# First halves of two units' states moved ahead of a scan's end, in an S5 + SwiGLU layer on one Trainium2 core

## The chip, the cores and the metric

The kernel runs on one core of one Trainium2 chip. The metric is the device time of one execution in microseconds (us); of several executions the median is taken. The engines are TensorE (PE; its weight loads are listed as PEld), VectorE (DVE), ScalarE (ACT), GpSimd (POOL) and SyncE (SP, which only issues DMA transfers here). ACT and POOL issue DMA transfers too; such an issue is listed under the engine's queue (ACTq, SPq).

## The reference, cut to what matters

The layer takes 1024 latent tokens and 256 context tokens of 1024 channels. It normalises and modulates them, runs a bidirectional S5 mixer, applies GELU and a gated linear unit (GLU), adds the residual, and then runs a SwiGLU feed-forward block (FFN) and a last norm. The S5 mixer has 64 groups of 16 channels; each group has 64 complex states per direction:

```
def run(u, h0):
    bu = jnp.einsum('lgh,gnh->lgn', u, b_bar)
    bu = bu.at[0].add(lam_bar * h0)
    a = jnp.broadcast_to(lam_bar, bu.shape)
    _, h = lax.associative_scan(_linear_combine, (a, bu), axis=0)
    return jnp.einsum('lgn,ghn->lgh', h, c_mat).real, h[-1]
...
fc, fl = s5_direction(uc, ul, *p_fwd)
bc, bl = s5_direction(uc[::-1], ul[::-1], *p_bwd)
...
y = y + d_skip * h;  g = gelu(y);  out = g * sigmoid(g @ w_glu + b_glu)
```

The scan must finish before the last tokens of either direction have their states; GELU, the GLU and the FFN follow.

## The kernel before

**Tiling.** Eight neighbouring tokens make one column: 32 context columns and 128 latent ones. Within a column the eight tokens act on each other through a small lag matrix (a Toeplitz block); between columns only the states are carried. The 64 groups make eight units of eight groups, two units to each of four quarters q. `STQ[q]` holds the states of a quarter: 160 columns, real and imaginary part, 16 entries, of which eight belong to each unit. The output of unit k is the sum of two products on TensorE: the lag product of its inputs (`x_mm`, lines 940 to 950, weights `KQ`) and the products of its states with the matrices `CL[q]` (`states_mm`, line 925, for half of the 128 columns; `states_all`, line 938, for all).

**The scan.** `scan()` runs on VectorE, in 32 steps over odd columns 33 to 95 (two columns at a time) and then 63 steps over every column to 158. A step is two products and two sums, each for all quarters. The even columns up to 94, left out by the first 32 steps, are filled afterwards by `rot`: two products and two sums on 128x64 elements (four columns of one unit). The procedure `one()` takes one such operation from a list after each of the two sums of a step, so a step has two slots. The list holds quarters 0 and 2. GpSimd fills quarters 1 and 3 (`fill`, letter F), whole, in eight operations for each half.

**The order.** Everything around and behind the scan is written out by hand in two strings of short words, PROG1 and PROG2, which `run` executes word by word; each engine then works through its own instructions in that order. The letters that matter here:

- C: one of four parts of `CL[q]`, two products on GpSimd and a sum, which the table HOWS puts on GpSimd (E) or on TensorE with ScalarE copying the result back (P, line 672). C32 and C33 are the last two parts of quarter 3.
- K: the lag products of half a quarter (`k_mats`, lines 812 to 820) into the banks `kt` and `pm`, two copies on ScalarE (line 824) and two writes to DRAM from ScalarE's queue.
- T: a load of one `KQ` from there, on SyncE's queue (line 833).
- R, Z, z: a copy of the backward states in turned order: first half (R, line 905, ScalarE), last half (Z) or both (z, line 907 on VectorE, line 905 on ScalarE).
- P: `x_mm` and the first half's states of a unit, into two of three banks `pw`. Y: the copy of the result into `Y` (line 996, ScalarE).
- N: the last half's states; D: VectorE adds them to `Y`. H: GELU. Q: for units 6 and 7, `x_mm` and both halves' states at once.
- I, J: transposes of `Y` for the GLU (line 1054) with the copy and the subtraction that split them in two parts; g: products of the GLU (lines 1095 to 1097).

PROG1 stands beside the scan and PROG2 behind it, and between the two all PSUM pools are closed and a new one (`pe`, eight banks) is opened. Units 0 to 5 have their first half in PROG1; units 6 and 7 come whole in PROG2.

Of the kernel before, what the change touches and what calls it, by code (L numbers as in the profile page):

```python
# [13 lines left out]
AF = mybir.ActivationFunctionType  # L14
# [3 lines left out]
P = 128  # L18
# [24 lines left out]
def s5_ffn_kernel(tc, a, out):  # L43
# [3 lines left out]
    with ctx:  # L47
# [879 lines left out]

        def states_all(k, pts, hs):

            for a_ in range(4):  # L930
                for ri in range(2):
                    for d in range(2):
                        for c in range(2):
                            cs_ = slice(64 * c, 64 * c + 64)
                            for gp in range(2):
                                ps = slice(64 * gp, 64 * gp + 64)
                                st = hs[ps, cs_, ri, a_] if d else STQ[k // 2][ps, 31 + 64 * c:95 + 64 * c, ri, 8 * (k % 2) + a_]
                                PE.matmul(flat(pts[gp][cs_, a_]), st, flat(CL[k // 2][ps, ri, d, 4 * (k % 2) + a_]),
                                          start=False, stop=a_ + ri + d == 5)

        def x_mm(k, pool):
# [10 lines left out]
        inner = {}  # L952
        HSe = [view(r, kb, [64, 2, 4]) for r, kb in ((RC[3], 14), (RC[3], 12), (RC[3], 14), (RC[3], 12), (RA, 2), (RA, 0))]
        HSl = [view(RA, STB * (i // 3) + 4.125 + 2 * (i % 3), [64, 2, 4]) for i in range(6)]
        HSq = {6: view(RA, 0, [P, 2, 4]), 7: view(RA, STB, [P, 2, 4])}

        def run(prog):


            for w in prog.split():  # L960
# [18 lines left out]
                elif op == "F":  # L979
                    fill(*divmod(i, 10), *((RW, 0) if i >= 30 else (RC[3], 12)))  # L980
                elif op == "T":
# [3 lines left out]
                elif op == "Z":  # L985
                    turned(i, 1, HSl[i], ENG[ZEN[i]])
                elif op == "z":
                    turned(i, 2, HSq[i], ENG[ZEN[i]])
                elif op == "P":
                    inner[i] = x_mm(i, pw)  # L990
                    states_mm(i, inner[i], 0, HSe[i], False)
                elif op == "Q":
                    inner[i] = x_mm(i, pe8)
                    states_all(i, inner[i], HSq[i])
                elif op == "Y":
                    S.copy(yview(i // 2, i % 2), inner[i // 2][i % 2])
                elif op == "N":
                    late[i] = [pe8([4, T, HC]) for _ in range(2)]
                    states_mm(i, late[i], 1, HSl[i], True)
                elif op == "D":  # L1000
                    for gp, po in enumerate(late[i]):
                        tt(yview(i, gp), po, yview(i, gp), ADD)
                elif op == "H":
                    if i in late:
                        S.activation(Y[:, i], Y[:, i], AF.Gelu_apprx_tanh)
                    else:
                        for gp in range(2):
                            S.activation(yview(i, gp), inner[i][gp], AF.Gelu_apprx_tanh)
                elif op == "I":
# [761 lines left out]
```

## Time and profile before

| | |
|---|---|
| median of 3 runs | 1016.06 us (1015.48 to 1016.09) |
| profiled execution | 1014.43 us |
| its span, first to last instruction | 1012.6 us |
| mean granted TensorE clock | 0.988 |
| busy: PE, DVE, POOL, ACT | 960.8, 778.9, 761.1, 438.5 us |

The profiled execution is 1.8 us longer than its span. A granted clock of 1.00 is TensorE's full 2.4 GHz and 0.50 is 1.2 GHz. The trace shows two records for each matmul on these 32-bit numbers: the 32 matmuls of half a unit's states are 64 records. The record of a matmul contains its way out of the array, so that neighbouring records overlap; the time that a series takes is read from start to start.

### The profile page before, as it was taken

The numbers are of one execution on the slowest core, as the hardware profiler recorded it, in microseconds if no ns is written. First come the engines' busy times: TensorE is split into PE (matmuls) and PEld (weight loads), VectorE is DVE, ScalarE is ACT, GpSimd is POOL, SyncE is SP. The second block draws the span as 40 slices with busy tenths as digits, with TensorE's granted clock in tenths as the row PEclk, the third lists the DMA queues.
The fourth block names the chain that finished last, engine by engine and source line by source line (L and its number), as shares of the span: only waits on it lengthen the run. The fifth ranks groups of instructions, "written<-read, shape, count | busy, mean of one in ns | idle before, by whom it ended". The sixth has DMA issues, their size and how long they took to land. (4 is left out here: it accounts for less than half of the span.)

```text
span 1012.6 us, 18558 instructions
## 1 busy us (share of the span) xinstructions
PE 960.8 (95%) x6988; PEld 771.8 (76%) x6988; DVE 778.9 (77%) x1642; ACT 438.5 (43%) x858; POOL 761.1 (75%) x586
## 2 busy tenths in 40 slices
PE   5987799799999999999999999999999999999996
PEld 1465423589999988778888888888888888888885
DVE  7979799995366867877958677686958677686987
ACT  5487622325444663443343343324343343424337
POOL 5799899993662448979785878777786877777774
PEclk9999999898999999999999999999999999999999
DMA  9765997324512021011212111121212111121205
GB/s 336 280 135 98 312 325 240 95 80 138 188 48 79 1 105 63 28 44 45 73 42 83 42 52 42 50 66 53 73 42 83 43 47 47 45 70 53 73 22 166
DMA packets 48546, 98.96 MB, mean 98 GB/s; under 512 B 4284, under 2 KB 18876, under 8 KB 47176
## 3 DMA queue, kind: packets, MB, share of 16 engines
q1 hardware_dynamic: 43272, 86.64, 25.7%
q0 software_dynamic: 2016, 7.34, 3.8%
q10 hardware_dynamic: 3168, 3.79, 1.1%
q8 instruction: 55, 0.90, 0.4%
q14 instruction: 35, 0.29, 0.1%
HBM read 84.25 MB, written 6.17 MB: 89 GB/s over the span
## 5 line engine op out<-in xcount | busy, mean ns | idle before, releaser
L77 POOL TENSOR_TENSOR c<-rxc,c 128x512 fp32r<-128x512 f32 x128 | 166.6, 1316 | 53.5 <-ACT c L1225 52.6
L1285 PE MATMUL ut<-ra,c 128*128 128x512 f32 x400 | 155.7, 389 | 1.2 <-DVE ra L77 1.2
L1284 PE MATMUL ut<-ra,c 128*128 128x512 f32 x400 | 155.7, 389 | 0.2 <-ACT ra L1225 0.2
L1286 PE MATMUL ut<-ra,c 128*128 128x512 f32 x400 | 155.6, 389 | 0.0
L1225 ACT CAST c<-rxc 128x512 fp32r<-128x512 f32 x128 | 79.0, 622 | 146.7 <-PE xt L1579 53.3
L1579 PE MATMUL xt<-c,c 128*128 128x512 f32 x540 | 129.7, 389 | 0.0
L77 DVE TENSOR_TENSOR ru<-ru,xt 128x1024 f32<-128x1024 f32 x90 | 107.9, 1216 | 13.4 <-PE xt L1579 9.4
L1579 PEld LDWEIGHTS xt<-c,c 128*128 128x128 f32 x540 | 101.4, 188 | 21.0
L77 DVE TENSOR_TENSOR ru<-ut,ru 128x512 f32<-128x512 f32 x98 | 67.2, 686 | 43.0 <-PE ut L1286 37.5
L1285 PEld LDWEIGHTS ut<-ra,c 128*128 128x128 f32 x400 | 75.1, 188 | 17.1 <-POOL rxc L77 1.5
L1284 PEld LDWEIGHTS ut<-ra,c 128*128 128x128 f32 x400 | 75.1, 188 | 16.1 <-ACT ra L1225 0.6
L1286 PEld LDWEIGHTS ut<-ra,c 128*128 128x128 f32 x400 | 75.1, 188 | 15.5
L77 POOL TENSOR_TENSOR c<-rw,c 128x512 fp32r<-128x512 f32 (+1 forms) x29 | 39.8, 1373 | 37.5 <-ACT c L1225 37.5
L77 POOL TENSOR_TENSOR c<-ru,c 128x512 fp32r<-128x512 f32 (+1 forms) x39 | 58.8, 1507 | 10.1 <-ACT c L1225 5.7
L1284 PE MATMUL ut<-c,c 128*128 128x512 f32 x160 | 62.3, 390 | 0.8 <-DVE rxa L77 0.8
L77 POOL TENSOR_TENSOR rxc<-rxc 128x512 f32<-128x512 f32 x40 | 61.5, 1537 | 1.6
L1286 PE MATMUL ut<-c,c 128*128 128x512 f32 x160 | 62.3, 389 | 0.0
L1285 PE MATMUL ut<-c,c 128*128 128x512 f32 x160 | 62.2, 389 | 0.0
L1579 PE MATMUL ut<-c,c 128*128 128x512 f32 x216 | 51.9, 389 | 0.0
L77 DVE TENSOR_TENSOR pe<-pe,ru 128x256 f32<-128x256 f32 x64 | 27.4, 428 | 29.5 <-ACT pe L1125 17.4
L584 PE MATMUL pv<-ru,c 128*64 128x160 f32 x512 | 42.3, 305 | 7.2 <-POOL ru L77 2.5
L77 DVE TENSOR_TENSOR ru<-ru,ut 128x512 f32<-128x512 f32 x76 | 47.3, 681 | 0.3
(440 smaller groups left out, 2571.2 us busy)
## 6 DMA issues: line engine op xcount, KB each, us to landing
c<-in_ada_w SPq DMA_DIRECT2D x46, 256.0 KB
rxc<-in_w SPq DMA_DIRECT2D x38, 256.0 KB
rxc<-in_w SPq DMA_DIRECT2D x19, 512.0 KB
ru<-in_w SPq DMA_DIRECT2D x11, 512.0 KB
rw<-in_w SPq DMA_DIRECT2D x11, 512.0 KB
ra<-in_ada_w SPq DMA_DIRECT2D x10, 512.0 KB
ra<-in_ada_w SPq DMA_DIRECT2D x18, 256.0 KB
ru<-in_xT SPq DMA_DIRECT2D x4, 1024.0 KB
```

Of the source, the lines that this page charges most:

```text
L77: eng.tensor_tensor(out=o, in0=x, in1=y, op=op)
L584: PE.matmul(pv[64 * (i % 2):64 * (i % 2) + 64, ri, c0:c0 + 160], w[:, i, 64 * ri:64 * ri + 64], U[:, 8 * b + 4 * j + i], start=True, stop= ...
L1225: S.copy(o[0], x)
L1284: PE.matmul(pu, wh, bh, start=start, stop=False)
L1285: PE.matmul(pu, wh, bl, start=False, stop=False)
L1286: PE.matmul(pu, wl, bh, start=False, stop=stop)
L1579: PE.matmul(pd, w[:, cs_], b, start=j in (1, 2, 4) and n == 0, stop=n == 2, skip_group_check=j not in (1, 2, 4))
```

## The change

- PROG1 gains the first half's states of units 6 and 7: new words R6, p6, Y12, Y13 and R7, p7, Y14, Y15. The word p is `states_mm` without `x_mm`. Unit 7's result goes to a place of its own (`Y7`), since `Y` still lies over inputs that unit 6 needs.
- In PROG2 units 6 and 7 go through N and D: N is `x_mm` and the last half's states for these two, D the sum on VectorE, H one GELU. Q, z, `states_all` and `HSq` go. The buffers of the turned states get new places (`HSe`, `HSl`), of which some are shared by R and Z words.
- F30 and F31 go. Of quarter 3's fills, unit 6's and the first half of unit 7's go into the scan's slots (12 more fills, 48 operations), behind quarter 2's, which now run unit by unit; the rest is f7, four operations on GpSimd behind C33.
- The sum of C32 goes from GpSimd to TensorE (HOWS).
- K3 stands directly behind K2; unit 2's `x_mm` (X2) ahead of K4 and K5, its states (S2) behind them; K6 ahead of p7 and K7 behind Y15; M2 and m0 (modulation columns) ahead of R5; T12 to T15 at the end of PROG1.

```
-HOWS = "PPPP PPEE PEEE EEEE"
+HOWS = "PPPP PPEE PEEE EEPE"
 PROG1, from M1 on:
-K2 R0 P0 Y0 Y1 K3 L3 R1 C20 P1 Y2 Y3 T4 T5 G3 T6 T7 C21 C22 C23 K4 K5 R2 P2 Y4 Y5 R3 P3 Y6 Y7 T8 T9 T10 T11
-C30 C31 R4 P4 Y8 Y9 C32 C33 R5 P5 Y10 Y11 K6 K7 M2 m0 F30 F31
+K2 K3 R0 P0 Y0 Y1 L3 R1 C20 P1 Y2 Y3 T4 T5 G3 T6 T7 C21 C22 C23 R2 X2 K4 K5 S2 Y4 Y5 R3 P3 Y6 Y7 T8 T9 T10 T11
+C30 C31 R4 P4 Y8 Y9 C32 C33 f7 M2 m0 R5 P5 Y10 Y11 R6 p6 Y12 Y13 R7 K6 p7 Y14 Y15 K7 T12 T13 T14 T15
 PROG2:
-Z0 N0 Z1 Z2 D0 Z3 N1 D1 Z4 H0 H1 N2 D2 H2 T12 T13 T14 T15 N3 Z5 D3 H3 N4 D4 z6 z7 I0 J0 I1 J1 ... Q6 H6 I4 J4 Q7 b0 I5 J5 H7 g03 ...
+Z0 N0 Z1 Z2 D0 Z3 N1 D1 Z4 H0 H1 N2 D2 H2 N3 Z5 D3 H3 N4 D4 Z6 Z7 I0 J0 I1 J1 ... N6 D6 H6 I4 J4 N7 D7 b0 I5 J5 H7 g03 ...
@@ scan
-            for j in range(8):
-                for d in range(2):
-                    rest.extend(fill_ops(2, d, j))
+            for k in range(4, 8):
+                for j in range(4 if k == 7 else 8):
+                    rest.extend(fill_ops(k // 2, k % 2, j))
@@ run
+                elif op == "f":
+                    fill(i // 2, 1, RW, 0, (8 * (i % 2),))
+                elif op == "p":
+                    inner[i] = [pw([4, T, HC]) for _ in range(2)]
+                    states_mm(i, inner[i], 0, HSe[i], True)
-                elif op == "Q":
-                    inner[i] = x_mm(i, pe8)
-                    states_all(i, inner[i], HSq[i])
-                    late[i] = [pe8([4, T, HC]) for _ in range(2)]
-                    states_mm(i, late[i], 1, HSl[i], True)
+                    late[i] = x_mm(i, pe8) if i > 5 else [pe8([4, T, HC]) for _ in range(2)]
+                    states_mm(i, late[i], 1, HSl[i], i < 6)
```

## Rows read from the trace of the kernel before

**Rows 1.** Busy time of each engine by stage (us, PE, PEld, DVE, ACT, POOL, PEclk, DMA)

```profile
228.00:262.00 34.00, 33.55 (x773) 32.55 (x761) 15.06 (x25) 15.72 (x23) 15.08 (x13) 0.92 0.57 174
...
360.00:470.00 110.00, 107.54 (x479) 88.08 (x478) 84.35 (x133) 48.72 (x90) 85.77 (x61) 1.00 0.18 63
470.00:1000.00 530.00, 530.00 (x2340) 438.84 (x2339) 401.11 (x472) 204.21 (x362) 403.68 (x300) 1.00 0.17 56
```

**Rows 2.** Timeline of DVE in the scan (start, us, engine, line, operands)

```profile
127.09 0.30 DVE L77 TENSOR_TENSOR ltb<-ra,lta 128x128 f32<-128x128 f32 x1
...
128.14 0.30 DVE L77 TENSOR_TENSOR ltb<-ra,lta 128x128 f32<-128x128 f32 x1
...
132.34 0.29 DVE L77 TENSOR_TENSOR ltb<-ra,lta 128x128 f32<-128x128 f32 x1
...
133.39 0.29 DVE L77 TENSOR_TENSOR ltb<-ra,lta 128x128 f32<-128x128 f32 x1
...
226.65 0.29 DVE L77 TENSOR_TENSOR ra<-ltc,ra 128x128 f32<-128x128 f32 x1
```

**Rows 3.** Groups of DVE instructions, 127 to 227 us (busy, mean ns, idle before)

```profile
L77 DVE TENSOR_TENSOR ltb<-ra,lta 128x128 f32<-128x128 f32 x95 | 27.4, 288 | 1.1
...
L77 DVE TENSOR_TENSOR lta<-ra,lta 128x64 f32<-128x64 f32 x64 | 13.8, 215 | 0.0
```

**Rows 4.** Timeline of ACT: copies of R5, of P5's, K6's and K7's results

```profile
218.61 0.63 ACT L905 COPY ra<-ra 128x512 f32<-128x512 f32 x1
222.35 1.07 ACT L996 COPY ru<-pw 128x512 f32<-128x512 f32 x2 [3.10 <-PE pw L925]
224.00 0.36 ACT L824 COPY r<-kt 128x240 f32<-128x240 f32 x1 [0.57 <-PE pm L820]
...
228.42 0.36 ACT L824 COPY rw<-kt 128x240 f32<-128x240 f32 x1 [3.31 <-PE pm L820]
```

**Rows 5.** PE by source line in short stretches: L938, L948, L925, L672 (us, PE, PEclk, DMA)

```profile
247.00:251.40 4.40, 4.25 (x128) 1.00 0.00 0
...
245.00:247.10 2.10, 1.93 (x16) 1.00 0.20 74
...
220.00:222.40 2.40, 2.28 (x64) 1.00 0.48 172
...
183.00:187.00 4.00, 3.70 (x8) 1.00 0.29 82
```

**Rows 6.** Timeline of DVE: sums D0, D1, D2 behind N0, N1, N2

```profile
232.59 1.29 DVE L77 TENSOR_TENSOR ru<-pe,ru 128x512 f32<-128x512 f32 x2 [3.66 <-PE pe L925]
...
235.03 1.29 DVE L77 TENSOR_TENSOR ru<-pe,ru 128x512 f32<-128x512 f32 x2 [0.82 <-PE pe L925]
237.01 1.29 DVE L77 TENSOR_TENSOR ru<-pe,ru 128x512 f32<-128x512 f32 x2 [0.69 <-PE pe L925]
```

**Rows 7.** PE alone, one us at a time (us, PE busy, PEclk, DMA)

```profile
194.00:195.00 1.00, 0.00 (x0) 1.00 0.57 173
...
196.00:197.00 1.00, 0.63 (x66) 0.52 0.09 25
...
226.00:227.00 1.00, 0.17 (x9) 0.88 0.38 124
```

**Rows 8.** Groups of PE instructions, 195 to 262 us (busy, mean ns, idle before)

```profile
L948 PE MATMUL pw<-ra,ru 128*128 128x128 f32 x64 | 10.7, 324 | 2.1 <-issue 1.4 <-ACT ru L996 0.7
...
L812 PE MATMUL kt<-c,rxa 64*16 64x112 f32 x120 | 6.1, 300 | 4.7 <-POOL c L77 3.5 <-ACT r L824 0.9 <-issue 0.3
```

**Rows 9.** Timeline of POOL: the sums of C32 and C33, and F31's last two

```profile
212.03 2.37 POOL L77 TENSOR_TENSOR c<-c,ra 128x1024 f32<-128x1024 f32 x1
...
218.45 2.38 POOL L77 TENSOR_TENSOR c<-c,rw 128x1024 f32<-128x1024 f32 x1
...
231.68 1.54 POOL L77 TENSOR_TENSOR ra<-ra,rw 128x256 f32<-128x256 f32 x2
```

**Rows 10.** Timeline of SP's queue: T12 to T15

```profile
231.30 4.16 SPq L833 DMA_DIRECT2D ra<-kd  x4
```

More of the change, by code (lines that the diff above doesn't have):

```diff
@@ L29 @@
 MAGIC = 12582912.0
-HOWS = "PPPP PPEE PEEE EEEE"
+HOWS = "PPPP PPEE PEEE EEPE"
 ZEN = "VVSVSVSV"
-PROG1 = ("A22 B0 A26 C02 G1 A30 A34 C03 A40 K0 A44 A48 C10 K1 L2 A54 G2 C11 A60 F10 C12 F11 C13 T0 T1 T2 T3 A64 M0 M1 K2 R0 P0 Y0 Y1 K3 L3 R1 C20 P1 Y2 Y3 T4 T5 G3 T6 T7 C21 C22 C23 K4 K5 R2 P2 Y4 Y5 R3 P3 Y6 Y7 T8 T9 T10 T11 C30 C31 R4 P4 Y8 Y9 C32 C33 R5 P5 Y10 Y11 K6 K7 M2 m0 F30 F31")
-PROG2 = ("Z0 N0 Z1 Z2 D0 Z3 N1 D1 Z4 H0 H1 N2 D2 H2 T12 T13 T14 T15 N3 Z5 D3 H3 N4 D4 z6 z7 I0 J0 I1 J1 w0 w1 l1 H4 N5 D5 I2 J2 H5 I3 J3 W0 W1 x0 x1 x2 x3"
-         " Q6 H6 I4 J4 Q7 b0 I5 J5 H7 g03 g13 I6 J6 g23 g05 g15 I7 J7 V1 w20 w21 g26 x10 x11 x12 x13")
+PROG1 = ("A22 B0 A26 C02 G1 A30 A34 C03 A40 K0 A44 A48 C10 K1 L2 A54 G2 C11 A60 F10 C12 F11 C13 T0 T1 T2 T3 A64 M0 M1 K2 K3 R0 P0 Y0 Y1 L3 R1 C20 P1 Y2 Y3 T4 "
+         "T5 G3 T6 T7 C21 C22 C23 R2 X2 K4 K5 S2 Y4 Y5 R3 P3 Y6 Y7 T8 T9 T10 T11 C30 C31 R4 P4 Y8 Y9 C32 C33 f7 M2 m0 R5 P5 Y10 Y11 R6 p6 Y12 Y13 R7 K6 p7 Y14 Y15 K7 T12 T13 T14 T15")
+PROG2 = ("Z0 N0 Z1 Z2 D0 Z3 N1 D1 Z4 H0 H1 N2 D2 H2 N3 Z5 D3 H3 N4 D4 Z6 Z7 I0 J0 I1 J1 w0 w1 l1 H4 N5 D5 I2 J2 H5 I3 J3 W0 W1 x0 x1 x2 x3"
+         " N6 D6 H6 I4 J4 N7 D7 b0 I5 J5 H7 g03 g13 I6 J6 g23 g05 g15 I7 J7 V1 w20 w21 g26 x10 x11 x12 x13")
 LOG2E = 1.4426950408889634
@@ L867, in scan, with fill @@
                 one()
-        def fill(q, h, reg, kb):
+        def fill(q, h, reg, kb, es=(0, 8)):
             tmps = [view(reg, kb + i, [256]) for i in range(2)]
             st, c0 = STQ[q], 32 * h
-            for e in (0, 8):
+            for e in es:
                 rot(st[:, 32 + c0:63 + c0:2, :, e:e + 8], st[:, 31 + c0:62 + c0:2, :, e:e + 8], LS[:, 0], 16 * q + e, E, tmps)
@@ L926, in states_mm @@
                                       start=start and ri == 0, stop=ri == 1 and (start or a_ == 3))
[L928 to L939, printed above, removed]
         def x_mm(k, pool):
@@ L952, in s5_ffn_kernel @@
         inner = {}
-        HSe = [view(r, kb, [64, 2, 4]) for r, kb in ((RC[3], 14), (RC[3], 12), (RC[3], 14), (RC[3], 12), (RA, 2), (RA, 0))]
-        HSl = [view(RA, STB * (i // 3) + 4.125 + 2 * (i % 3), [64, 2, 4]) for i in range(6)]
-        HSq = {6: view(RA, 0, [P, 2, 4]), 7: view(RA, STB, [P, 2, 4])}
+        HSe = [view(r, kb, [64, 2, 4]) for r, kb in ((RC[3], 14), (RC[3], 12), (RC[3], 14), (RC[3], 12), (RA, 2), (RA, 0), (RA, 4), (RA, 6))]
+        HSl = [view(RA, (4, 6, 0)[i] if i < 3 else STB * (i // 3) + 4.125 + 2 * (i % 3), [64, 2, 4]) for i in range(8)]
+        Y7 = [view(RA, 8 + 2 * i, [4, T, HC]) for i in range(2)]
         def run(prog):
@@ L986, in run @@
                     turned(i, 1, HSl[i], ENG[ZEN[i]])
-                elif op == "z":
-                    turned(i, 2, HSq[i], ENG[ZEN[i]])
                 elif op == "P":
@@ L991, in run @@
                     states_mm(i, inner[i], 0, HSe[i], False)
-                elif op == "Q":
-                    inner[i] = x_mm(i, pe8)
-                    states_all(i, inner[i], HSq[i])
+                elif op == "X":
+                    inner[i] = x_mm(i, pw)
+                elif op == "S":
+                    states_mm(i, inner[i], 0, HSe[i], False)
+                elif op == "p":
+                    inner[i] = [pw([4, T, HC]) for _ in range(2)]
+                    states_mm(i, inner[i], 0, HSe[i], True)
                 elif op == "Y":
-                    S.copy(yview(i // 2, i % 2), inner[i // 2][i % 2])
+                    S.copy(Y7[i % 2] if i > 13 else yview(i // 2, i % 2), inner[i // 2][i % 2])
                 elif op == "N":
-                    late[i] = [pe8([4, T, HC]) for _ in range(2)]
-                    states_mm(i, late[i], 1, HSl[i], True)
+                    late[i] = x_mm(i, pe8) if i > 5 else [pe8([4, T, HC]) for _ in range(2)]
+                    states_mm(i, late[i], 1, HSl[i], i < 6)
                 elif op == "D":
                     for gp, po in enumerate(late[i]):
-                        tt(yview(i, gp), po, yview(i, gp), ADD)
+                        tt(yview(i, gp), po, Y7[gp] if i == 7 else yview(i, gp), ADD)
                 elif op == "H":
[L1004 to L1008, printed above, removed]
+                    S.activation(Y[:, i], Y[:, i], AF.Gelu_apprx_tanh)
                 elif op == "I":
```

2 lines of the change are left out of this document (1 added, 1 removed).

## The prediction

> **What bounds the kernel now.** I read the busy time by stage first. From 470 to 1000 us TensorE is busy all 530.00 us, from 360 to 470 it misses 2.5 us, from 228 to 262 it misses 0.45 [rows 1]. Behind about 228.8 us, then, the time is the moment at which TensorE begins PROG2 plus the work it has from there on; a microsecond of TensorE work taken out behind that point is a microsecond of the result, and what VectorE, ScalarE and GpSimd do there has room.
>
> Next I asked the timelines what sets that moment. VectorE's scan begins at 127.09 and its last sum ends at 226.65 + 0.29 = 226.94: 95 steps [rows 2, 3] of 1.051 us, without a gap. N0 needs the last columns and Z0, a copy that takes VectorE not quite 1 us more, so 228 is the earliest. TensorE itself is then busy with K7; its copy out of bank `kt` runs at 228.42 for 0.36 us [rows 4], and N0 begins right behind it, at 228.83. So two chains end almost together: the scan (228.0) and TensorE's queue in PROG1 (228.8). Work moved from behind the join to ahead of it is free only as far as that second chain has slack.
>
> **The change part by part.**
>
> *The states taken out of PROG2.* A Q issues 64 state matmuls, 4.25 us; half of them, as P and N have, take 2.28 (64 records) [rows 5]. Both numbers hold the same way out of the array, so the difference, 1.97, is clean. Two units: -3.9 us behind the join. The lag products (1.93 us each, 16 records [rows 5]) stay there. D6 and D7 are new on VectorE, 1.29 us each [rows 6], and H6 and H7 wait for them; what needs H6 and H7 are I6 and I7, which stand behind N7 and several g words, so TensorE has other work. Z6 and Z7 copy half of what z6 and z7 copied. Cost on the path: nothing; if that cover were gone, 1.3 us a unit.
>
> *The clock behind the join.* N0's result reaches VectorE at 232.59, N1's at 235.03, N2's at 237.01 [rows 6]: 3.7, 2.4 and 2.0 us. In the 1 us table the granted clock drops during 226 to 227, when TensorE had worked 0.17 us of that microsecond [rows 7]; the stage's mean is 0.92 [rows 1]. So N0 and part of N1 ran at 1.2 GHz, and against N2's 2.0 they lost 1.7 + 0.4 = 2.1 us. In the new order p6, K6, p7 and K7 follow each other with no wait of theirs longer than about 1.7 us, and the clock should be at full when N0 begins: -2.1. Bounds: 0 (it drops anyway) and -2.1; I take -2.1, because what stood ahead of the drop, a queue of K6 and K7 that waited for each other's banks, is now filled by p7.
>
> *The start of N0.* I add up TensorE's queue ahead of the join. Up to K4 little changes: K4 waits 3.5 us for GpSimd's last part of quarter 2 [rows 8], with TensorE idle from 192 to 195 [rows 7], and X2 (1.9 us) fits in that hole. K3 directly behind K2 has to wait for K2's copies, about 2 us, which the same hole takes up. With X2 gone from behind K5, and the clock not down (it fell at 196, right after the hole [rows 7], and units 2's and 3's products ran slow), P4 should end about 211.5.
>
> C32 then needs GpSimd's products. GpSimd's sum of C32 began at 212.03 [rows 9], so they are there at 212.0, and nothing ahead of them on GpSimd is changed. From there: C32's sum on TensorE 3.5 (a sum of this kind: 3.70 with its tail [rows 5]); P5 4.1 (1.9 + 2.2); then a hole, since p6 has no lag products to cover the copies ahead of it on ScalarE: Y10 and Y11 1.07 and R6 0.63 [rows 4], 1.7; p6 2.0; K6 1.7 (from the end of P5's states, just ahead of the copies at 222.35, to 224.00 [rows 4]); p7 2.1; K7 1.7; its first copy 0.4. 212.0 + 17.2 = 229.2. C33 on GpSimd ends 2.37 earlier, at 218.4 instead of 220.8, ahead of p6, which needs it, and f7 (four operations, about 3 us by F31's two in 1.54 [rows 9]) ends at 221.5, ahead of R7. R6 and R7 need the fills: the list is emptied two a step, unit 6's at about 215 and unit 7's at 224, both ahead of their R.
>
> This sum has no reserve for stalls that the trace calls "issue": 1.4 us ahead of P2 and 0.3 within the K words [rows 8], both behind dense runs of K. The new order has such runs too, so I add 1.1: N0 at 230.3, +1.5. Bounds: 228.3 (the scan alone, -0.5) and 232 (every stall and a longer wait, +3.2).
>
> *The fills in the scan.* 48 operations more on VectorE, whose scan is one of the two chains. An empty step lasts 128.14 - 127.09 = 1.05 us, a step with two of these operations 133.39 - 132.34 = 1.05 [rows 2]: they fall into the time in which a step's two sums wait for each other. The list holds 8 + 112 = 120 operations at the start of the 63 steps, which have 126 slots. So 0. Bounds: 0 and 48 x 0.215 (mean of one [rows 3]) = 10.3 us, were none hidden. I take 0 by the two steps, the nearest rows there are. The Trainium skill says otherwise in general (VectorE: DVE Perf Modes, "The TRN2 errata"): each operation pays a fixed latency, 58 cycles beside its elements at 0.96 GHz, so that small ones are dear; by it 48 operations of 64 elements would be an estimated 6.1 us, N0 at 234.1 and the time 1015.3. The trace does not bear that out here: the latency is already paid by the step's own wait.
>
> *The rest.* F30 and F31 off GpSimd, M2 and m0 earlier: no one waits for them before or after. T12 to T15 take SyncE 4.16 us, from 231.30 [rows 10]; now from about 232.5, so they are in place at some 238 to 239, and N6 wants them at 244: nothing, with 5 us to spare. The loads behind them on that queue come 1 us later, also covered.
>
> *Sum.* -3.9 - 2.1 + 1.5 = -4.5 us. The profiled execution goes from 1014.43 to 1009.9 and its span from 1012.6 to 1008.1. The runs' median is 1016.06, 1.6 above that execution; the same difference on it gives **1011.5 us**.
>
> **The rivals.**
>
> *The clock stays down at the join.* For it: it dropped there before, after holes no longer than the 1.7 us ahead of p6. Against: that hole comes five microseconds earlier, with dense work behind it. -3.9 + 1.5 = -2.4: 1013.7.
>
> *The queue ahead of C32 is late.* If the clock falls in 196 to 206 as before, K5, S2 and P3 run at half rate and P4 ends about 3 us after C32's products: N0 at some 233.3, -3.9 - 2.1 + 4.5 = -1.5: 1014.6.
>
> *Slower: TensorE's queue in PROG1 becomes the bound.* It gets 64 state matmuls and C32's sum, some 7.7 us, just ahead of the join. If the clock falls in the hole ahead of p6 and stays low, p6 and p7 cost 1.7 more each (as N0 did) and K6 and K7, by the same ratio, 1.4 each: 6.2. N0 then begins at 236.5 and N0 and N1 are slow as before: +7.7 - 3.9 = +3.8: 1019.9. It decides once N0 is later than 228.8 + 3.9 = 232.7 with a slow start, or 234.8 with a fast one. For it: the chain has no slack left by my own sum. Against: units 3 to 5, a run as dense as p6 to K7, waited 0.7 us in all for their banks [rows 8], and the stalls that I know of are in the sum.
>
> *The fills lengthen the scan.* At 10.3 us N0 begins at 228.0 + 10.3 = 238.3: +9.5 - 3.9 - 2.1 = +3.5, 1019.6. It decides from 6.8 us on. Against it stands the equal length of the two steps. The page named above would put the time between, at no gain.
>
> *No change: the GLU waits.* g03 needs W0, split on GpSimd, and I0 to I3. Should it start where it did before, all that is gained ahead is lost there: 1016.1. Against: GpSimd is busy 15.08 of 34 us in that stage [rows 1], and its part of W0 hangs on N5 and J3, which come earlier too.
>
> **How the numbers follow.** Chances: my forecast 0.58, its own range 1009.0 to 1013.2 (N0 at 228.3 to 232); clock down at the join 0.14; late ahead of C32 0.12; slower by TensorE's queue 0.07; longer scan 0.03; no change 0.06. The range of 8 in 10 takes in the first three: 1009.0 to 1014.9. A measurement of this kernel tells about 0.2%, 2.0 us. Faster by more than that: the first two, all of them, and half of the third, 0.78; within it: the other half and no change, 0.12; slower 0.10.
>
> **What would show it.** Right: steps of 1.05 us to the scan's end at 226.9; N0 near 230; D0, D1, D2 two microseconds apart; the granted clock at 1.00 from 196 on; N6 and N7 near 4 us each; TensorE without gaps behind. Wrong: a scan step above 1.05; a wait on ScalarE's R6 or R7 or on GpSimd's C32 longer than 2 us; a clock of 0.50 between 220 and 234; a gap at g03.

## The result, and the profile after

The changed kernel takes 1017.76 us (median of 22 runs, 1015.07 to 1021.36), the kernel before 1015.82 us (22 runs on the same chip, 1012.64 to 1019.11): ratio 1.0022, 95% interval 1.0012 to 1.0031. It is slower by 1.9 us, where the prediction said 4.5 us faster. The profiled execution's span is 1016.4 us, that of before 1012.6.

Busy time by stage, with the columns of [rows 1] and [rows 7]:

```profile
196.00:197.00 1.00, 1.00 (x104) 1.00 (x102) 1.00 (x7) 0.00 (x0) 1.00 (x1) 1.00 0.03 8
226.00:227.00 1.00, 1.00 (x46) 0.88 (x48) 0.93 (x5) 0.19 (x1) 0.00 (x0) 1.00 0.06 16
228.00:262.00 34.00, 29.00 (x823) 26.93 (x810) 15.79 (x28) 15.76 (x23) 7.04 (x4) 1.00 0.43 132
470.00:1000.00 530.00, 530.00 (x2340) 438.87 (x2339) 400.28 (x469) 202.81 (x358) 406.11 (x301) 1.00 0.17 55
```

The clock is where the prediction wanted it: 1.00 at 196 and at 226, where before had 0.52 and 0.88, and a mean of 1.00 in 228 to 262. The last stage is that of before. What is new stands in the third line: TensorE is busy for 29.00 of 34 us, where before it was busy for 33.55.

VectorE's timeline, in the scan and behind it, answers to [rows 2, 6]:

```profile
127.80 0.30 DVE L78 TENSOR_TENSOR ltb<-ra,lta 128x128 f32<-128x128 f32 x1
...
128.85 0.30 DVE L78 TENSOR_TENSOR ltb<-ra,lta 128x128 f32<-128x128 f32 x1
...
187.87 0.28 DVE L78 TENSOR_TENSOR ltb<-ra,lta 128x128 f32<-128x128 f32 x1
...
188.92 0.28 DVE L78 TENSOR_TENSOR ltb<-ra,lta 128x128 f32<-128x128 f32 x1
...
227.91 0.29 DVE L78 TENSOR_TENSOR ra<-ltc,ra 128x128 f32<-128x128 f32 x1
...
237.65 1.29 DVE L78 TENSOR_TENSOR ru<-pe,ru 128x512 f32<-128x512 f32 x2 [5.97 <-PE pe L926]
...
239.65 1.29 DVE L78 TENSOR_TENSOR ru<-pe,ru 128x512 f32<-128x512 f32 x2 [0.37 <-PE pe L926]
241.66 1.29 DVE L78 TENSOR_TENSOR ru<-pe,ru 128x512 f32<-128x512 f32 x2 [0.73 <-PE pe L926]
```

A step of the scan lasts 1.05 us without fill operations (127.80 to 128.85) and with them (187.87 to 188.92). D0, D1 and D2 are 2.0 us apart, so N1 and N2 run at full clock. The scan ends at 228.20 instead of 226.94. Of these 1.26 us 0.71 lie ahead of it: it begins at 127.80 instead of 127.09, and over kernels with the same words up to there its beginning lay anywhere from 126.9 to 129.6. The other 0.55 are its own length (100.40 instead of 99.85): one step, from 212.1, lasts 1.41 us in after and in every other run with the changed scan, with a wait of 0.3 in it, and 24 more steps with fills are about 0.01 longer each.

What follows is counted from the scan's end. N0 begins 5.67 us behind it (before: 1.89), g03 28.12 us behind N0 (before: 29.36), the last matmul 746.03 behind g03 (before: 746.12). The change costs 0.55 in the scan and 3.78 ahead of N0, gives 1.24 between N0 and g03, and does nothing after that: +3.1 in this pair of traces up to the last matmul, +1.9 by the medians.

What TensorE waited for from 195 to 262 us (engine, tile, line, what ended the wait: us in total, times, the longest) shows where it went. Of after:

```profile
PE pe L926 <- issue: 2.5, 2, 1.4
PE pw L936 <- DMA ra<-kd: 2.0, 2, 1.3
PE pm L821 <- issue: 1.9, 2, 1.4
PE pe L936 <- issue: 1.2, 1, 1.2
...
PE kt L821 <- issue: 0.4, 1, 0.4
```

Of before, the same view:

```profile
PE kt L812 <- POOL c L77: 3.5, 1, 3.5
PE pw L948 <- issue: 1.4, 1, 1.4
PE kt L812 <- ACT r L824: 0.9, 2, 0.5
...
PE pm L812 <- issue: 0.8, 1, 0.8
```

The reader is to see two things. "Issue" (a wait for nothing that the profile shows) has grown from 2.5 us to more than 6, and 3.7 of it (`pe`, lines 926 and 936) lies behind N0, where before had none. And the wait for GpSimd is replaced by one for the loads T8 and T9 (`ra<-kd`), in P4. TensorE's timeline puts them in their places:

```profile
201.55 0.17 PE L821 MATMUL pm<-rxc,rxa 64*16 64x16 f32 x1 [1.42 <-issue]
...
209.98 1.13 PE L936 MATMUL pw<-ra,ru 128*128 128x128 f32 x8 [1.26 <-DMA ra<-kd]
...
215.16 1.12 PE L673 MATMUL pw<-c,r 128*128 128x512 f32 x2
...
224.53 1.75 PE L926 MATMUL pw<-c,ra 64*64 64x128 f32 x48 [0.52 <-ACT ra L906]
228.60 0.17 PE L821 MATMUL kt<-rxc,rxa 64*16 64x16 f32 x1 [0.45 <-issue]
232.15 0.27 PE L813 MATMUL kt<-c,rxa 64*16 64x112 f32 x1 [0.36 <-issue]
233.87 0.98 PE L926 MATMUL pe<-c,ra 64*64 64x128 f32 x20 [0.47 <-ACT rw L825]
235.99 1.26 PE L926 MATMUL pe<-c,ra 64*64 64x128 f32 x33 [1.14 <-issue]
245.63 0.64 PE L926 MATMUL pe<-c,ra 64*64 64x128 f32 x13 [1.40 <-issue]
253.17 1.72 PE L936 MATMUL pe<-ra,ru 128*128 128x128 f32 x13 [1.19 <-issue]
```

C32's sum on TensorE (line 673) begins at 215.16; GpSimd's timeline has its products done at 212.75, so TensorE is 2.4 us late for it.

Counted in the trace, the "issue" waits lie 256 TensorE instructions apart, or a multiple of that (a matmul record and its weight load are two), each 1.3 to 1.5 us behind the end of a packet of 16 KB on DMA queue q8, "instruction", 55 of which run in the whole execution. The view of DMA queues of after, 226 to 238 us (packets, MB, share of 16 engines), has four of them:

```profile
q8 instruction: 4, 0.07, 2.1%
```

Theories. *Supply*: TensorE's instructions come in blocks of 256, and where they are used up faster than the next block comes, it stalls; the change put more small matmuls into such a stretch. *Queue*: the order of the words does it (T8 and T9 late, the hole ahead of p6, C32 on TensorE), and the stalls are a side matter. Both were put to the chip.

### The profile page after: what moved, and what is told of

It is laid out like the page before. It is cut to its first block, busy times and chain, and to the rows that moved or that the text cites. A ratio compares the mean times of both kernels' runs of the same rounds, so it can differ in the third digit from the quotient of the medians.

```text
span 1016.4 us, 18619 instructions
## 1 busy us (share of the span) xinstructions
PE 961.8 (95%) x6996; PEld 771.8 (76%) x6996; DVE 781.9 (77%) x1694; ACT 442.8 (44%) x864; POOL 750.1 (74%) x573
## 5 line engine op out<-in xcount | busy, mean ns | idle before, releaser
L585 PE MATMUL pv<-ru,c 128*64 128x160 f32 x512 | 44.5, 312 | 5.6 <-ACT rxa L389 1.8
```

The lines of the kernel that those rows point to most:

```text
L585: PE.matmul(pv[64 * (i % 2):64 * (i % 2) + 64, ri, c0:c0 + 160], w[:, i, 64 * ri:64 * ri + 64], U[:, 8 * b + 4 * j + i], start=True, stop= ...
```

## The experiments

In the table, "scan" is the end of VectorE's last sum, "N0" TensorE's start of it behind that, "g03" its start behind N0, all in us from one trace each; the ratio is that of the medians to the kernel before on the same chip, with its 95% interval.

| kernel | scan | N0 | g03 | ratio to before |
|---|---|---|---|---|
| before | 226.94 | +1.89 | +29.36 | 1 |
| after | 228.20 | +5.67 | +28.12 | 1.0022 (1.0012 to 1.0031) |
| e1_q_kept | 228.99 | +2.46 | +29.78 | 1.0029 (1.0016 to 1.0042) |
| e2_shift32 | 231.11 | +7.58 | +25.49 | 1.0057 (1.0042 to 1.0073) |
| e3_states_first | 227.54 | +6.88 | +27.56 | 1.0023 (1.0010 to 1.0037) |
| e4_k_ahead | 227.41 | +5.61 | +26.02 | 1.0021 (1.0004 to 1.0038) |
| e5_loads_late | 227.47 | +6.61 | +28.45 | 1.0097 (1.0079 to 1.0116) |
| e6_whole_block | 227.62 | +7.23 | +26.47 | 1.0032 (1.0018 to 1.0047) |
| e7_half_block | 228.69 | +5.46 | +23.43 | 1.0007 (0.9990 to 1.0025) |
| e8_before_half | 226.81 | +3.03 | +28.01 | 0.9992 (0.9981 to 1.0003) |
| e10_k_short | 228.00 | +3.33 | +23.37 | 0.9982 (0.9963 to 1.0001) |
| e11_k_ahead_half | 228.42 | +4.75 | +25.61 | 1.0017 (1.0002 to 1.0033) |
| e12_k_between | 227.86 | +9.14 | +24.55 | 1.0048 (1.0031 to 1.0065) |
| e14_c32_on_gpsimd | 228.15 | +4.18 | +26.20 | 0.9989 (0.9974 to 1.0004) |
| e15_t_late | 227.59 | +6.58 | +27.30 | 1.0028 (1.0015 to 1.0041) |
| e18_gpsimd_k_ahead | 227.69 | +4.98 | +25.17 | 0.9996 (0.9978 to 1.0014) |
| e19_gpsimd_half | 230.04 | +5.25 | +23.61 | 0.9989 (0.9974 to 1.0004) |
| e20_gpsimd_k_half | 227.46 | +2.90 | +26.86 | 0.9999 (0.9985 to 1.0014) |

Three of these tell how much one trace is worth. e5, e6 and e15 have after's TensorE words up to N0, with the borders of the blocks on the same words, and their N0 is at +6.61, +7.23 and +6.58 against after's +5.67. A difference in N0 of 1.6 us between two traces can be scatter. The 22 executions of after have spans from 1013.0 to 1019.3 us, so the span of one trace says little about a kernel. e9 and e13, not in the table, were run once each and are read only for what their dense runs show.

**First four: one part undone, the borders moved, two orders.**

```diff
 e1: -R5 P5 Y10 Y11 R6 p6 Y12 Y13 R7 K6 p7 Y14 Y15 K7 T12    (and Z6 Z7, N6 D6, N7 D7)
     +R5 P5 Y10 Y11 K6 K7 T12                                 (and z6 z7, Q6, Q7)
 e2: +for _ in range(32): PE.matmul(psx[:, 0:8], blk, ident[:, 0:8])     ahead of the first matmul
 e3: -R4 P4 Y8      +R4 q4 Y8            (q: the states first, x_mm, which needs T8 and T9, behind them)
 e4: -R6 p6 Y12 Y13 R7 K6 p7 Y14 Y15 K7
     +R6 K6 p6 Y12 Y13 R7 K7 p7 Y14 Y15
```

> The changed kernel with units 6 and 7 whole in PROG2 again (words Q, z and states_all as before; no R6, p6, R7, p7); everything else of the change is kept: fills in the scan, C32's sum on TensorE, X2 ahead of K4, K3 behind K2, T12 to T15 at the end of PROG1. Theory 'supply' (TensorE stalls, called issue, every time its instruction stream crosses a block of 256 instructions faster than the next block is fetched): the 128 instructions of p6 and of p7 are gone ahead of N0, which starts within 1.5 us of the scan's end plus Z0, and behind N0 the 3.9 us of states come back while the issue stalls of 3.7 us mostly stay or move: 1015 to 1017 us. Theory 'queue' (TensorE's chain ahead of N0, through the late loads of KQ and the hole ahead of p6, is all of the loss): N0 some 4 us earlier, no stalls counted, and -3.9 us of states given back: equal to the changed kernel within 1 us, 1017 to 1018.5.

Measured: N0 at +2.46, g03 at +29.78, 1.0029; 1017.70 us, where 'queue' had it. Putting the states back gives 3.2 us ahead of N0 and takes 1.7 behind it, and the time does not move: the moved states, which were the point of the change, are worth nothing that these runs can tell. What else the change does is enough to make it slower.

> The changed kernel with 32 dummy matmuls of 8 columns at the start, in time in which TensorE waits for data; they are overwritten and cost nothing there. They move every later instruction of TensorE by 128 places (if each is four instructions) against the blocks of 256. Theory 'supply': the issue stalls of the trace (200.0 to 201.6, 234.6 to 236.0, 244.0 to 245.6, 251.7 to 253.2 us) move by half a block to other words, by about 2 us where the states run, and some vanish where the boundary falls on slow lag products: the time moves by 1 to 3 us either way, most likely down, 1014.5 to 1017. Theory 'queue': stalls and time as in the changed kernel, 1017.8 within 0.5.

Measured: the stalls moved to other words, still 256 instructions apart: 1.47 and 1.40 us ahead of N0, and at most 0.6 behind, so that g03 comes 25.5 behind N0 instead of 28.1, although the clock is at 0.50 there from 239.7 to 243.1. This is for the supply. The 32 matmuls themselves cost some 3 us ahead of the scan, where they stand in the way, so the time says nothing.

> The changed kernel with unit 4's states ahead of its lag products (which need the loads T8 and T9, on which TensorE waited 1.26 and 0.76 us). Theory 'queue': P4 ends 2 us earlier, C32's sum begins at GpSimd's products, and N0 and the end come 2 us earlier: 1015.8. Theory 'supply': N0 earlier by up to 2 us, but as the fetches keep their own pace part of it turns into issue stalls at the block boundaries: 1016 to 1017.5.

Measured: the wait for T8 and T9 is gone and N0 is no earlier (+6.88, within the 5.67 to 7.23 of after's words); stalls of 2.07 in K5, 1.42 behind N0 and 2.26 stand instead. Against the queue as the whole cause.

> The changed kernel with K6 ahead of p6 and K7 ahead of p7 (R6 and R7 stay where they are on ScalarE), so that K6 and K7 cover the copies that p6 and p7 wait for (1.6 us ahead of p6) and N0 no longer waits for K7's copy (0.5 us). Theory 'queue': N0 and the end 2 us earlier, 1015.8. Theory 'supply': K6 stands directly behind P5 and the holes in which blocks arrived are gone; the stalls within K6 and K7 grow (0.45 and 0.36 now) and the gain is 0.5 to 1.5 us: 1016.3 to 1017.3.

Measured: N0 at +5.61, no earlier; this trace's span is 1013.4, the median of the times stays that of after (1.0021). A stall of 1.30 now lies at 225.8, in p6 behind the K that moved into the hole, and one of 1.12 in K7.

**The borders moved at no cost, and the loads.** The added matmuls now stand ahead of A64, where TensorE waits for a load anyway, and write places that K2 overwrites.

```diff
+ elif op == "j":
+     for _ in range(i):
+         PE.matmul(kt[0:HC, 0:8], blk[:, 0:HC], ident[:, 0:8], start=True, stop=True)
 e6: -T3 A64   +T3 j64 A64     256 instructions
 e7: -T3 A64   +T3 j32 A64     128
 e8: the same as e7 in the kernel before
 e5: -I1 J1 w0 w1 l1 H4 ... I3 J3 W0 W1 x0 x1 x2 x3 N6 D6 H6 I4 J4 N7 D7 b0
     +I1 J1 H4 ... I3 J3 w0 w1 l1 N6 D6 H6 I4 J4 N7 D7 W0 W1 x0 x1 x2 x3 b0
```

> After, with 64 matmuls of 8 columns on rows that K2 overwrites, ahead of A64, where TensorE waits 2.7 us for a load anyway: 256 TensorE instructions more, one whole block. Theory 'supply' (stalls at every 256th instruction): the borders between blocks fall on the same words of the program as in after, so the stalls stay with the same words (each 256 later by count), N0 is 5 to 6.5 us behind the scan's end and N0 to g03 27.5 to 28.7; the time is that of after within 1 us. Theory 'queue' says the same of the time, but gives no reason for stalls to lie 256 apart. It also tells what the added instructions cost by themselves: nothing is expected.

> As the run with 64 matmuls ahead of A64, with 32: 128 instructions, half a block, at the place where TensorE waits anyway, so without the 3 us that the 32 matmuls at the start of the kernel cost ahead of the scan. Theory 'supply': stalls as in the run with 32 at the start, at 3984, 4240, 5259 and 5515 ahead of N0 and next to none behind it: N0 7 to 8 us behind the scan's end, N0 to g03 25.2 to 26, the time 0 to 1.5 us under after. Theory 'queue' (only the order of the words counts): the same as after, N0 to g03 28 and N0 at +5.7.

Measured: with a whole block the stalls sit in the same words as in after (at 228.5 and 232.3 ahead of N0, at 235.6 behind it), and the ratio, 1.0032, is that of after. N0 is later than expected (+7.23) and g03 closer (+26.47), for the stalls that after has at 245.6 and 253.2 did not come. But the clock of e6 is at half for 3.4 us behind N0 (window, us, PE busy, PEclk, DMA share):

```profile
237.40:240.80 3.40, 3.40 (x72) 0.50 0.32 70
```

With half a block N0 is at +5.46, sooner than expected. The ratio is 1.0007, with an interval (0.9990 to 1.0025) that overlaps that of after, so that the time alone does not tell the two apart; this trace's span is 1012.0, although work was added. TensorE's waits of e7 from 226 to 262 us:

```profile
PE kt L821 <- issue: 1.2, 1, 1.2
PE pw L926 <- issue: 0.7, 1, 0.7
PE pe L926 <- ACT rw L825: 0.5, 1, 0.5
```

There is no "issue" behind N0, and g03 follows it after 23.43 us. The prediction's two gains there, 3.9 and 2.1, taken from the 29.36 of before, give 23.36: without the stalls they come whole.

> The kernel before with the same 32 matmuls ahead of A64. Theory 'supply': before has no stall behind N0 (its N0 and N1 run at half the clock, slower than the blocks come) and 1.4 and 0.8 ahead; with the borders 128 instructions off they hit other words, so its N0 moves by up to 1.5 us either way, and N0 to g03 goes up by 0 to 1.5 from 29.4. Theory 'queue': before stays at +1.9 and 29.4, time within 0.7 us of before.

Measured: N0 1.1 us later, as expected; g03 1.35 us closer, where up to 1.5 more was expected; 0.9992. The stall of 0.8 that before has at 226.0, just ahead of the fall of its clock, is elsewhere (1.8 us, up to 225.4). The clock falls with it: TensorE alone, one us at a time, falls to 0.50 within that stall and is at full again by 232.

```profile
224.00:225.00 1.00, 0.00 (x0) 0.94 0.00 0
225.00:226.00 1.00, 0.29 (x18) 0.50 0.00 0
...
231.00:232.00 1.00, 1.00 (x30) 0.64 0.23 70
232.00:233.00 1.00, 1.00 (x43) 1.00 0.25 80
```

In before the clock falls at 226.8 and is back at 234. The fall that the change was to cure at the join came with a stall at a border in both, and moved with it.

> After, with the loads of the weights w0, w1 and l1 moved from behind I1, J1 to behind I3, J3 (they stand ahead of H4 there no more), and the splits W0, W1 and x0 to x3 behind N7, D7. Behind N0 TensorE then shares the DMA engines with fewer weights while its states run. Theory 'traffic' (the blocks of 256 TensorE instructions come late because weight loads and T12 to T15 fill the DMA engines): the two stalls of 1.40 and 1.19 at instructions 6025 and 6278 shrink to under 0.5 together, N0 to g03 goes from 28.1 to about 25.8, and the time falls by some 2.2 us, unless g03 then waits for W0. Rival 'pace' (a block takes longer to come than the states take to issue, whatever else is on the DMA engines): the stalls stay at 1.2 to 1.5 each, N0 to g03 27.5 to 28.5, time within 0.5 us of after.

Measured: much slower, for a cost that the expectation named only in passing: TensorE's waits from 228 to 275 us have g03 waiting for W0, and what follows it for the same splits on GpSimd.

```profile
PE pe L926 <- issue: 2.6, 2, 1.7
PE pe L1084 <- POOL c L78: 2.4, 1, 2.4
PE pe L1083 <- DVE c L1061: 1.5, 1, 1.5
```

Behind g03 the kernel then takes 750.2 us instead of 746.0. The first of the two stalls stayed (2.0 us between the records), the second went. But this says nothing about the traffic, for the loads did not move: SyncE issues w0, w1 and l1 from 240.56 in e5 and from 241.31 in after, right behind T12 to T15 in both.

**The supply by itself.**

```diff
 e9:  -T3 A64   +T3 j512 A64
 e13: +for _ in range(9 if (q, hq) == (1, 0) else 1):      around the matmuls of K2
```

> After, with 512 of the same 8-column matmuls ahead of A64: 2048 TensorE instructions, eight blocks, in one dense run that waits for nothing. A measurement of the supply by itself. Theory 'rate' (in all ten traces so far no two fetches of a block of 256 TensorE instructions begin less than 3.3 us apart, however dense the work): the run takes 8 x 3.4 = 27 us less about one block that is there already, 24 us; the fetches are 3.3 to 3.8 apart, and a stall called issue stands every 256 instructions. Rival 'pace' (the instructions themselves are that slow, and the fetches only lie beside): at the pace of the K words, 128 instructions in 0.75 us, the run takes 12 us, with no regular stalls.

Measured: the fetches are 3.4 to 3.8 apart as expected, and the run takes 26.8 us. But its records come smoothly but for two gaps of 0.5 and 0.3, 25 ns apart at first and 27 later, and 256 instructions at 27 ns a pair are 3.45 us: these matmuls are by themselves as slow as the limit. The run tells nothing apart.

> After, with the matmuls of K2 issued nine times over (the same values into the same places; one set of copies): 2448 instructions in one run that waits for no engine, at the pace of the K words (272 in 1.7 us), which the 8-column matmuls of the run before did not reach (25 ns each, 40 records a microsecond). Theory 'rate' (a block of 256 TensorE instructions can't be entered sooner than 3.45 us after the one before it was entered: fetch begun 1.1 us behind the entry, 1.0 on the queue, 1.35 until the first instruction runs): the run lasts 28 to 33 us, with stalls of 1.4 to 2.0 at each of about nine borders, and fetches 3.4 to 3.6 apart. Rival 'pace': 9 x 1.7 = 15.3 us, no regular stalls.

Measured: the nine-fold K2 lasts from 173.5 to 209.4, 36 us, 20 more than 9 times 1.7, a little above what 'rate' gave. The beginnings behind the stalls, of TensorE's timeline:

```profile
180.63 0.17 PE L822 MATMUL kt<-rxc,c 64*16 64x16 f32 x1 [1.88 <-issue]
...
184.09 0.18 PE L818 MATMUL kt<-r 64*16 64x16 f32 x1 [1.99 <-issue]
...
187.54 0.34 PE L814 MATMUL kt<-c,c 64*16 64x112 f32 x1 [1.16 <-issue]
...
191.00 0.34 PE L814 MATMUL kt<-c,c 64*16 64x112 f32 x1 [1.08 <-issue]
```

They are 3.46, 3.45 and 3.46 us apart; the five that follow, up to 209.09, are 3.45, 4.00, 3.73, 3.46 and 3.45 apart. The busy time of TensorE within two of these blocks (window, us, PE busy with its records, PEclk, DMA share):

```profile
180.63:181.91 1.28, 1.27 (x128) 1.00 0.05 13
181.91:184.09 2.18, 0.20 (x25) 0.62 0.00 0
184.09:185.99 1.90, 1.90 (x127) 0.50 0.03 9
185.99:187.54 1.55, 0.39 (x14) 0.50 0.00 0
```

128 matmuls with their weight loads run in 1.27 us at full clock and then nothing begins for 2.18; the next 128 take 1.90 us at half the clock, and the stall is 1.55. The sum is the same, the DMA engines are nearly idle. This settles it: in this dense run a block of 256 instructions costs 3.45 us at the least, at either clock. The fetch of the next begins 1.0 to 1.2 us behind the entry into the one before (1.5 and 1.6 where the block took 3.73 and 4.00), is 1.0 us on the queue, and its first instruction runs 1.3 to 1.5 us after.

**What follows from that rate.**

```diff
 e10: K6 and K7 without the sums of line 821     (- for d in range(2)   + for d in range(2 if q < 3 else 0))
 e11: the edits of e4 and e7 together
 e12: -R5 P5 Y10 Y11 R6 p6 Y12 Y13 R7 K6 p7 Y14 Y15 K7
      +R5 K6 P5 K7 Y10 Y11 R6 p6 Y12 Y13 R7 p7 Y14 Y15
```

> After, with the diagonal sums over the states left out of the lag products K6 and K7 (64 records of 16 columns each; the output lacks that part): 128 instructions and about 0.75 us of TensorE less in each, 256 instructions in all, so the borders behind K7 stay on the same words. Theory 'rate': N0 begins earlier by about the time of one fetch, 3.0 to 3.8 us (5.7 behind the scan's end becomes about 2.3, or as early as Z0 lets it), and the time falls by 3 or more. Theory 'queue' (TensorE's own work and its waits for copies set N0): earlier by the 1.5 us of busy time, N0 at +4.2, time 1.5 less.

Measured: N0 at +3.33, 2.3 us earlier than in after and 3.2 to 3.9 earlier than in e5, e6 and e15, which is more than the 1.5 of the busy time and about the 3.4 of a block. Behind N0 no "issue" is left, and g03 comes after 23.37 us, as in e7. 1.5 us of work left out lower the time by 0.4%, 4 us, against after, with intervals that do not meet (0.9963 to 1.0001, 1.0012 to 1.0031); the span of this trace is 1009.1.

> After, with K6 ahead of p6 and K7 ahead of p7, and the half block of 32 matmuls ahead of A64: both edits that helped alone. Theory 'rate': K6 behind the hole finds a block ready, and the borders fall well: span 1010.5 to 1012.5 (12.0 with the half block alone), ratio to before 0.997 to 1.000. Theory 'queue': only the order of the words counts: that of K ahead alone, 1013.4.

> After, with the words ordered so that the dense ones (K, 272 instructions in 1.7 us) stand between loose ones: R5 K6 P5 K7, then p6 and p7. K6 follows the sum of C32 (few instructions in 3.5 us) and K7 fills the hole of 1.9 us ahead of p6. Theory 'rate': 960 instructions from C32's end at 215.2 + 3.5 = 218.7, of which some 256 are there: 704 / 256 x 3.4 = 9.4 us at the least, 11.5 us of work: N0 at 230.2 to 231.5 instead of 233.9, 2.4 to 3.7 earlier; span 1012.7 to 1014. Theory 'queue': 11.5 us of work and no hole: 230.2, too; told apart by the stalls in K6 and K7, which rate puts under 0.5 each.

Measured: both missed, with ratios of 1.0017 and 1.0048. In e11 N0 comes at +4.75, but stalls of 0.8 in K6 and 1.4 in p7 stand ahead of it and one of 1.6 comes back behind it. In e12 the supply does what was expected: TensorE's waits from 205 to 240 us have no "issue" at all.

```profile
PE pw L926 <- ACT ru L988: 2.5, 2, 1.8
PE pw L926 <- ACT ra L906: 0.9, 2, 0.5
```

But the order makes a wait of its own. K7's two copies stand on ScalarE ahead of Y10 and Y11, so p6 waits for Y11 from 227.4 to 229.2, and in that hole the clock falls:

```profile
228.00:229.00 1.00, 0.00 (x0) 1.00 0.37 123
229.00:230.00 1.00, 0.66 (x2) 0.69 0.37 123
```

p6 ends at 233.5, two more copies and R7 are waited for, and N0 is at +9.1. That is the prediction's slower rival, a hole ahead of p6 that takes the clock down, in a kernel made here and not in after.

**What is left of the queue.**

```diff
 e14: -HOWS = "PPPP PPEE PEEE EEPE"     +HOWS = "PPPP PPEE PEEE EEEE"
 e15: -K7 T12 T13 T14 T15  ...  H2 N3     +K7  ...  H2 T12 T13 T14 T15 N3
 e18: the edits of e14 and e4;  e19: those of e14 and e7;  e20: all three
```

> After, with the sum of C32 back on GpSimd (the table HOWS as before). TensorE loses 3.5 us of work with few instructions, between P4 and P5. Theory 'rate': those 3.5 us were not what held N0, since the blocks for K6 to p7 come no faster for it; C33, and f7 behind it, come 2.4 us later on GpSimd, R6 and R7 with them; N0 at +5 to +7, span within 1.5 us of after's. Theory 'queue' (TensorE's own work ahead of N0 is the bound): up to 3.5 us earlier, N0 at about +2.5, span 1013.

Measured: the theory of the rate missed. With C32's sum on GpSimd P5's products begin at 215.91 instead of 218.70, N0 at +4.18, 1.5 earlier than in after and 2.4 to 3.1 earlier than in e5, e6 and e15, and the time falls to 0.9989 of before, 0.33% under after, with intervals that do not meet. So those 3.5 us of TensorE work did lie on the path. 0.85 of stall in K6 and again in K7 (records' gaps; 0.6 each in after) took half a microsecond of it back. The rest of the span's 3.5 us lies behind N0, where one stall fewer fell.

> After, with T12 to T15 (1 MB on SyncE's queue) issued behind H2 again, as in the kernel before, instead of at the end of PROG1. Theory 'traffic on the fetch' (the fetch for the block that is entered at 245.6 began 3.1 us behind its forerunner's entry at 240.0 instead of 1.1, while T12 to T15 filled the DMA engines): the stall of 1.4 to 1.7 there goes or shrinks to under 0.5, N0 to g03 is about 26.5 instead of 28.1, unless the next border, beside the weights w0, w1 and l1, takes more. Rival: the traffic is the same and only later (the stall moves to the next border): N0 to g03 28 to 29.5. N6 may then wait for T12: up to 1 us.

Measured: the stall is there still (2.3 us between the records), its fetch beginning 3.7 us behind the entry into the block before, and N6 did not wait. But the edit moved next to nothing: SyncE issues T12 to T15 from 236.34 in after and from 236.65 in e15. The theory was not put to the test, and e15 is in effect a second trace of after.

> After with two edits that took its time down alone: the sum of C32 back on GpSimd (span 1012.9, from 1016.4), and K6 ahead of p6, K7 ahead of p7 (1013.4). In the first alone C33's sum ends at 221.5 and K6 begins at 224.6, so K6 can go ahead of p6, into the hole of 220.8 to 222.4. Theory 'queue' (TensorE's own words and its waits): N0 1 to 1.6 us earlier than at +4.2, span 1011 to 1012, ratio to before 0.997 to 0.999. Theory 'rate' (the number of instructions between P5 and N0, at 3.45 us a block, is the same): N0 at +3.5 to +5, span 1012 to 1014, ratio 0.998 to 1.001.

> After with the sum of C32 back on GpSimd and the half block of 32 matmuls ahead of A64, which moves the borders of the blocks by 128 instructions. Theory 'rate': stalls move to other words, the time by up to 2 us either way from 1014.4, N0 to g03 between 23.4 and 28. Theory 'queue': no change by the half block: 1014.4 within 0.7.

> All three: C32's sum on GpSimd, K6 and K7 ahead, and the half block. Theory 'rate': N0 at +3.5 to +5, N0 to g03 23.4 to 26.5, span 1009.5 to 1013. Theory 'queue': as the run without the half block.

Measured: no further gain. e18 and e20 are within 0.2% of before, with stalls of 1.2 to 2.1 in p6, K7 or p7; e19, with stalls of 1.5 and 1.6 in p7 and K7, is where e14 is. In e20 K6, moved ahead, also waits 1.8 for GpSimd's C33. N0 at +2.90 in e20 is the earliest of a whole computation with the states moved ahead, and the clock falls just behind it (0.50 from 231.5 to 234.9). The best, e14 and e19, are 0.11% under before with intervals that reach 1.0004. No version here is shown to beat the kernel before.

## Why the prediction was wrong

*Right.* The fills are nearly free: steps of 1.05 us, 88 records of each fill operation instead of 64, and 0.55 us on the whole scan, where 0 was taken and up to 10.3 allowed. Why one step lasts 1.41 was not found. The states' 3.9 us and the clock's 2.1 come whole between N0 and g03 where no block is late (23.4 in e7 and e10). Nothing waits for the GLU or behind it. T12 to T15 start 4 us later than forecast (236.34), at no cost. The clock is at full when N0 begins, in after as in e5, e6 and e15, but the reason given for it, that K6 and K7 no longer wait for each other's banks, is only part of it: ahead of its fall before (226.8) stands, beside such waits, an "issue" wait of 0.8 in K7, which [rows 8] leave out. That it stays up in after is in part luck: with the same words it is at 0.50 from 200.9 to 204.4 in e15, from 210.7 to 214.1 in e5 and, behind N0, from 237.4 to 240.8 in e6.

*The first step that failed* is in the start of N0: "P4 should end about 211.5". In after K5 stalls 1.4 us at a border (200.0 to 201.6), P4 waits 2.0 for the loads T8 and T9, for which the sum has no term, and C32's sum, right behind P4, starts 2.4 us behind its products, at 215.16 instead of 212.0. The wait is not the stall's doing: in e5 K5 stalls only 0.7 and P4 waits 2.5 for the same loads.

```profile
208.77 1.13 PE L936 MATMUL pw<-ra,ru 128*128 128x128 f32 x8 [1.69 <-DMA ra<-kd]
```

The chain is K5's last write to DRAM, the loads, P4. SyncE issues T8 2.3 us behind that write in before, 2.4 in after and 2.5 in e5; TensorE reaches P4 10.9 us behind it in before (212.85), where P2 and P3 stand whole in between, partly at half the clock, and 6.9 and 7.4 in after and e5, where X2 has gone ahead of K4. The step that was to make P4 early took away what covered its loads. From C32's sum to N0 the working had 17.2 and 1.1 for stalls; it measured 18.7 (215.16 to 233.87), so that part was sized about rightly. The rival of a late queue ahead of C32 had the place and the time of N0 (233.3), but not the cause, for the clock was not down. e14 shows that the sum of C32, put on TensorE, itself delays N0, by 1.5 in these two traces.

*The second, and larger,* is that the working has no term for "issue" behind the join. The scan's 0.55 and N0's 3.78 alone would have left -6.0 + 4.3 = -1.7: still faster, as by the prediction's own rule (slower from 234.8 on, with a fast start; N0 came at 233.87). The gain behind N0 was 1.24 instead of 6.0: the gaps at the three borders there are 1.4, 1.7 and 1.5 us between records, 4.6 in all. The prediction read [rows 8] as two stalls of 1.4 and 0.3 "behind dense runs of K", and took them as occasional; the third, of 0.8, it missed. They stand at borders, 256 instructions apart. Its argument that units 3 to 5 are "a run as dense as p6 to K7" holds for busy time and not for instructions: a P is 160 instructions in 4.1 us, while p6, K6, p7 and K7 are 800 in 7.5 us of the sum, for which blocks at 3.45 us would take 10.8. They took 9.3 (224.53 to 233.87), and part of them stood in a block that was there already. The slow N0 and N1 of before used 256 instructions in 6.1 us and had no stall.

*What the stalls behind N0 need in addition.* At full clock two words of N are 256 instructions in 4.0 us, slower than 3.45. They stall because the fetch begins late there. Over the traces of all 18 kernels other than e9 and e13, it begins mostly 0.9 to 1.6 us behind the entry where the words run without a wait and the other DMA traffic is small; in some 20 cases between 237 and 257 us in which the DMA engines were over 0.75 busy with other transfers in the meantime, it begins 1.7 to 5.3 us behind; at a share near 0.6, anywhere from 0.3 to 3.7. In after it was 3.1 (from 240.0) and 5.3 us (from 245.6). Beside it the windows of after from border to border show the DMA share (the last column but one):

```profile
235.98:239.98 4.00, 4.00 (x128) 3.99 (x128) 1.96 (x4) 2.42 (x3) 0.00 (x0) 1.00 0.32 81
239.98:245.64 5.66, 4.26 (x135) 4.06 (x131) 3.86 (x7) 2.84 (x4) 0.00 (x0) 1.00 0.71 199
245.64:253.16 7.52, 6.34 (x127) 5.74 (x126) 4.72 (x8) 4.70 (x8) 0.00 (x0) 1.00 0.63 233
```

That the traffic delays the fetch goes with these numbers, and no run took the traffic away or moved it (e5 and e15 were meant to, and left the loads where they were), so it is argued and not shown. With the borders 128 instructions off (e7) no delay was felt; but e6, with after's borders, had one stall there instead of three, so the place of the borders is not all of it.

The Trainium skill (Runtime: NRT & Kernel Launch, "Instruction fetch mechanics") says that an engine's instructions come in blocks of 256, fetched over a DMA queue of its own while the current block runs, and that crossing a border is mostly hidden. The trace agrees on the blocks (q8, 16 KB, stalls 256 apart). On the hiding it agrees where the words run slowly, from 470 to 1000 us, where some 18 blocks come and TensorE is busy all 530.00 us; in dense runs it does not: 1.4 to 2.2 us between records at every border in e13, 0.6 to 1.7 at six borders of after from 200 to 254.

*Still open:* how much of the 0.22% is the place of the borders and how much the order. Half a block more takes away what may be most of it (1.0007, interval up to 1.0025, so not told from after), C32 back on GpSimd all of it; together they add up to no more than the one.

## What to carry to other kernels

Count a stretch's TensorE instructions beside its busy time: matmuls and weight loads together, 256 to 3.45 us in these traces. Where small tiled matmuls run denser than that, moving more of them there is not free even if every engine has room, and "issue" waits that lie a fixed number of instructions apart are the sign of it. Before crediting an order with one or two microseconds in such a stretch, run it with half a block of harmless instructions ahead, and see whether the "issue" waits move to other words. Read from the trace, too, whether an edit that is to move a load moved it: a word further on in the program left it in its place here, twice.

## What the runs showed of the hardware

- In a dense run a block of 256 TensorE instructions is entered 3.45 us or more behind the one before it, at half the clock (e13) as at full (3.46 in e4, from 227.14 to 230.60). In all 20 traces the smallest distance between the beginnings of two fetches is 3.3 to 3.7 us. Right behind a wait of TensorE two entries can lie closer (226.00 and 228.60 in after), since the fetch began only 0.26 us behind the first.
- A stall can take the clock down: in e13 the granted clock goes from 1.00 to 0.50 in the course of the second stall of about 2 us (the windows above), in e8 within one of 1.8. In after it stays at 1.00 through the stall of 1.4 in K5.
- 128 instructions added ahead, where TensorE waits anyway, move the stalls to other words: g03 comes 23.4 us behind N0 in e7 and 28.1 in after (26.5 and 27.3 in e6 and e15). The time moved by 0.15%, which the intervals do not tell from nothing.
